# A decoder trunk whose split weight tiles lie at another shift in their buffers for each block of columns

## The chip, the cores and the metric

The kernel runs on one core of one Trainium2 chip. The metric is device time in microseconds (us), the median of repeated executions. Everything is float32, and no other core works beside it.

## The reference

The reference is a two-layer decoder trunk over 256 tokens of width 2048. Each layer has a mixing part (8 heads of sparse attention and 8 of stick-breaking attention, fed by one input projection and merged by one output projection) and a feed-forward part with a gate. Cut to what matters here:

```python
D_MODEL, SEQ, DEPTH, D_FF = 2048, 256, 2, 5632
for layer in range(DEPTH):
    xn = rms_norm(h, norm_mix[layer])
    h = h + hybrid_mixer(xn, ...)          # proj = xn @ w_in (2048 x 5656); ...; o @ w_out (2048 x 2048)
    xn = rms_norm(h, norm_ffn[layer])
    h = h + (silu(xn @ w_gate) * (xn @ w_up)) @ w_down    # 2048 x 5632, 2048 x 5632, 5632 x 2048
return rms_norm(h, norm_final)
```

The mixer also compresses keys and values by two small products (`w_cmp_k1`, `w_cmp_v1`, each 4096 x 256).

## The kernel before

All weights are read once, as 804 tiles of at most 128 x 1024 float32 (512 KB), in the order in which they are used (`plan`). A tile of 1024 columns holds two 512-column pieces for two steps of the inner dimension. Each tile goes through three stages, each in a ring of buffers:

- `load_next` (L150) has SyncE's queue bring tile i into one of `RAW` = 5 buffers `raw`. The load into a buffer waits until the split of the tile that was in it has been read to its end by VectorE.
- `split_next` (L159) cuts it into two parts whose sum is the float32 value and which TensorE multiplies in single passes: `hi` is a rounded copy by ScalarE (L165), `lo` the rest, `raw - hi`, by VectorE (L166). `hi` and `lo` have 4 buffers each. Up to `AHEAD` = 3 tiles are split ahead of the product that runs. Six tiles near the end are split into other places (`places`): buffers of `xh`/`xl` and `ah`/`al`.
- `mm` (L398) multiplies. The activations are the stationary operand, a 128 x 128 block of `xh`/`xl` (a transposed normalised input, split in the same way; for `w_down` it is `ah`/`al`), and the weights are the moving operand. For each 128 rows of weights and each half of the tokens three products go into the same accumulator: `xh*hi` (L409), `xh*lo` (L410), `xl*hi` (L411). `cmp_mm` (L540, L541) is the like for the two compressing products, with `fr`, 60 stationary columns per step, and 256 moving columns.

TensorE has one such stream of products from beginning to end. The attention, the norms and the transposes are generators, of which `step` runs one piece at every weight tile, so their instructions stand between the tiles' products. Instruction order is fixed by the program's text; no scheduler moves it.

Where the operands lie in a partition matters for this change. In the built program the tiles `xh`, `xl`, `raw`, `hi` and `lo` all start at addresses that leave 224 bytes when divided by 512; `ah` and `al` leave 96. Blocks and pieces inside the tiles start at multiples of 512 bytes, except in three kinds: the first block of columns of each layer is 280 wide, so its three pieces start 0, 1120 and 2240 bytes into the tile; the second is 256 wide; and step k of `fr` starts 240*k bytes into `fr`. In this document the *distance* of a product is the start of its moving operand less the start of its stationary operand, taken modulo 512. So `hi` with `xh` has distance 0, `hi` with `ah` has distance 128, the pieces of the first block have 0, 96 and 192, and `hi` with `fr` goes through all multiples of 16.

Of the kernel before, what the change touches and what calls it, by code (L numbers as in the profile page):

```python
# [8 lines left out]
F32R = mybir.dt.float32r  # L9
# [5 lines left out]
P = 128  # L15
# [9 lines left out]
EPS = 1e-6  # L25
NEG = -1e30
SCALE = 128 ** -0.5
EXPLN = "natural_log_exp_and_others"
SILU = "silu_and_others"

# the hidden columns of the feed-forward, in blocks of 512, are worked off in two parts
FF_PARTS = [(0, 6), (6, 11)]

# columns of the constants array
C_ID, C_NEG, C_CNEG, C_COK, C_D1, C_D0, C_MT, C_BM, C_INV, C_END = (
    0, 128, 384, 416, 448, 960, 1472, 1728, 1732, 1748)

# column blocks of the input projection, in the order in which they are computed
IN_CHUNKS = [
    ("ck", [(1024, 256), (2560, 24)]),  # L40
    ("cv", [(1280, 256)]),
# [20 lines left out]


def plan():
    """The tiles of one layer's weights in the order in which they are used."""

    def tiles(mat, name, cols, k1, k0=0):
        w = sum(c[1] for c in cols)
        step = max(1, min(4, 1024 // w))
        return [Item(mat, name, cols, list(range(k, min(k1, k + step))), k0, k1) for k in range(k0, k1, step)]  # L70

    main = {name: tiles("w_in", name, cols, KT) for name, cols in IN_CHUNKS}
    ck = tiles("w_cmp_k1", "wk", [(0, 256)], 32)
    cv = tiles("w_cmp_v1", "wv", [(0, 256)], 32)
    seq = []
    for name, _ in IN_CHUNKS:
        for j, t in enumerate(main[name]):
            seq.append(t)
            if name == "k" and ck and j >= 1:
                seq.append(ck.pop(0))  # L80
            elif name == "v" and j == 0:
                seq += ck
                ck = []
            elif (name == "v" and j >= 4) or name == "qn0":
                if cv:
                    seq.append(cv.pop(0))
    o = [tiles("w_out", f"o{c}", [(512 * c, 512)], KT) for c in range(4)]
    seq += o[0][:6] + o[1][:6] + o[0][6:] + o[1][6:] + o[2] + o[3]
    for c0, c1 in FF_PARTS:
        for c in range(c0, c1):  # L90
            for m, n in (("w_gate", "g"), ("w_up", "u")):
                seq += tiles(m, f"{n}{c}", [(512 * c, 512)], KT)
        for c in range(4):
            seq += tiles("w_down", f"d{c}", [(512 * c, 512)], 4 * c1, 4 * c0)
    off = 0
    for t in seq:
        t.off = off
        off += P * t.n
    return seq, off


def pi_parts(scale, bits, n):
    """2*pi*scale as n parts of `bits` leading bits each."""
    from fractions import Fraction
    rest = Fraction(2 * 314159265358979323846264338327950288419716939937510582097494459230781640628620899,
                    10 ** 80) * scale
    out = []
    for _ in range(n):
        e = 0
        while rest >= Fraction(2) ** (e + 1):  # L110
            e += 1
        while rest < Fraction(2) ** e:
            e -= 1
        q = Fraction(2) ** (e - bits + 1)
        part = (rest // q) * q
        out.append(float(part))
        rest -= part
    return out
# [3 lines left out]
def trunk(ctx: ExitStack, tc: tile.TileContext, x, positions, cst, gT, gfin, bgate, posT, w2, ws, out):  # L122
    nc = tc.nc
    V, A, T = nc.vector, nc.scalar, nc.tensor
    items, total = plan()
    seq = [(l, t) for l in range(DEPTH) for t in items]
# [4 lines left out]
    wp = ctx.enter_context(tc.tile_pool(name="wp", bufs=4))  # L131
# [10 lines left out]
    def o_ps():  # L142
        return ps.tile([P, 512], F32, tag="o", name="ops", bufs=1)

# [1 line left out]
    RAW, AHEAD = 5, 3  # L146
    raw, parts, places = {}, {}, {}
    ptr = [0, 0]

    def load_next():  # L150
        i = ptr[0]
# [7 lines left out]
    def split_next():  # L159
        i = ptr[1]  # L160
        n = seq[i][1].n
        r = raw.pop(i)
        hi, lo = places[i]() if i in places else (wp.tile([P, 1024], F32R, tag="hi", name="hi", bufs=4),
                                                  wp.tile([P, 1024], F32R, tag="lo", name="lo", bufs=4))
        A.activation(hi[:, :n], r[:, :n], AF.Copy)  # L165
        V.tensor_tensor(lo[:, :n], r[:, :n], hi[:, :n].bitcast(F32), op=OP.subtract)  # L166
        parts[i] = (hi, lo)
        ptr[1] += 1
# [6 lines left out]
        while ptr[0] < min(len(seq), ptr[1] + RAW):  # L175
            load_next()

# [1 line left out]
    active = []  # L179

    def spawn(g):
# [16 lines left out]

    flags = set()

# [1 line left out]
    cs = cp.tile([P, C_INV], F32, name="cs")  # L202
    inv = cp.tile([P, 16], F32, name="inv")
    gt = cp.tile([P, 3 * DEPTH, KT], F32, name="gt")
# [43 lines left out]
        nc.sync.dma_start(cs[:, P:], cst[:, P:C_INV])  # L248
        nc.sync.dma_start(w2t, w2)

# [1 line left out]
    cc = cp.tile([P, 3, 32], F32, name="cc")  # L252
    sn = cp.tile([P, 3, 32], F32, name="sn")

# [1 line left out]
    c2 = cp.tile([P, 3, 16], F32, name="c2")  # L256

    def angles():
        """positions * inv, brought into [-pi, pi] by an exact subtraction of whole turns."""
        G = nc.gpsimd  # L260
        MAGIC = 1.5 * 2.0 ** 23
        PI = 3.1415925
# [45 lines left out]
            A.activation(sn[:, :, sl], ang, AF.Sin, scale=2.0 * half - 1.0)  # L308

    def rope(X, tmp, idx, np_=P):  # L310
        """X [np_, n, 128], rotated in place by the tables' row idx."""
        n = X.shape[1]
        cb = cc[:np_, idx:idx + 1, :].to_broadcast([np_, n, 32])
        t = tmp[:np_, :2 * n * 32].rearrange("p (b n d) -> p b n d", b=2, n=n)
        V.tensor_tensor(t[:, 0], X[:, :, 0:32], cb, op=OP.mult)
        V.tensor_tensor(t[:, 1, :, 0:16], X[:, :, 16:32],
                        sn[:np_, idx:idx + 1, 0:16].to_broadcast([np_, n, 16]), op=OP.mult)
        V.tensor_tensor(t[:, 1, :, 16:32], X[:, :, 0:16],
                        sn[:np_, idx:idx + 1, 16:32].to_broadcast([np_, n, 16]), op=OP.mult)
        V.tensor_tensor(X[:, :, 0:32], t[:, 0], t[:, 1], op=OP.add)  # L320

# [1 line left out]
    def rsqrt_a(ss, v, r, count):  # L323
        V.tensor_scalar(v, ss, 1.0 / count, EPS, op0=OP.mult, op1=OP.add)

# [8 lines left out]
        V.tensor_tensor(r, r, q, op=OP.mult)  # L334

    class Norm:
        """1/rms of h per token, gathered block by block."""

        def __init__(self, parts=4):
            self.done = False  # L340
# [14 lines left out]
            rsqrt_c(v[:, :n], r, q[:, :n])  # L355
            self.done = True

# [1 line left out]
    def new_x():  # L359
        return [None] * 4  # L360

# [2 lines left out]
                xp.tile([P, 4, S], F32R, tag="xl", name="xl", bufs=5))  # L364

    def xt_block(X, c, srcs, g):
        """[tokens, 512 columns] times g per column, transposed into X[c]."""
        ts = []
        for t in range(2):
            src = srcs(t)  # L370
            pt = tmp_ps()
            for j in range(4):
                T.transpose(pt[:, j * P:(j + 1) * P], src[:, j * P:(j + 1) * P], ident)  # L373
            tv = tmp512().rearrange("p (a b) -> p a b", a=4)
            V.tensor_tensor(tv, pt.rearrange("p (a b) -> p a b", a=4),  # L375
                            g[:, 4 * c:4 * c + 4, None].to_broadcast([P, 4, P]), op=OP.mult)
            ts.append(tv)
        xh, xl = X[c]
        for t in range(2):
            A.activation(xh[:, :, t * P:t * P + P], ts[t], AF.Copy)  # L380
        for t in range(2):
            sl = slice(t * P, t * P + P)
            V.tensor_tensor(xl[:, :, sl], ts[t], xh[:, :, sl].bitcast(F32), op=OP.subtract)  # L383
# [12 lines left out]
        yield  # L396

    def mm(i, accs, X, ts=(0, 1)):  # L398
        """One weight tile: accs[t] += X^T[t] @ W, float32 by three passes."""
        it = seq[i][1]  # L400
        hi, lo = parts[i]
        for j, kt in enumerate(it.kts):
# [7 lines left out]
                T.matmul(o, a, lo[:, sl], start=False, stop=False)  # L410
                T.matmul(o, b, hi[:, sl], start=False, stop=(kt == it.k1 - 1))  # L411

    # =====================================================================
    norm = Norm()
    X = new_x()

# [25 lines left out]
    for l in range(DEPTH):  # L442
        g_mix, g_grp, g_ffn = gt[:, 3 * l, :], gt[:, 3 * l + 1, :], gt[:, 3 * l + 2, :]
        flags.clear()
        with ExitStack() as actx:
# [42 lines left out]
            flat = {}  # L488

            def c_chunk(which, accs):  # L490
                """Tokens of the compressed branch: transposed, cut into blocks, positions added."""
                while "prep" not in flags:
                    yield
                ns = []
# [101 lines left out]
                flags.add(which)  # L596

            def qk_chunk(name, accs):
                """Queries or keys: scaled, rotated where they are, transposed to [d, token]."""
                sc = rq if name[0] == "q" or name[:2] == "sq" else r  # L600
                ns = []
                for t in range(2):
# [26 lines left out]
                yield  # L629
                flags.add(name)  # L630

# [1 line left out]
            obank = {}  # L633

            def nsa_unit(g, rr, qi):
# [70 lines left out]
                         skip_group_check=True)  # L706

            def o_norm(qd, qi, o):
                """Each head's output over its root mean square."""
                if qd not in on:  # L710
                    on[qd] = big(f"on{qd}").rearrange("p (t d) -> p t d", t=2)
                dst = on[qd][:, qi]
# [40 lines left out]
                    yield from pipeline(us)  # L753
                flags.add("nsa")

# [1 line left out]
            def rev(a):  # L757
                s_, n_ = a.ap[-1]
                return bass.AP(tensor=a.tensor, offset=a.offset + (n_ - 1) * s_, ap=[*a.ap[:-1], [-s_, n_]])
# [49 lines left out]
            spawn(sb_driver(0))  # L809
            spawn(sb_driver(1))  # L810

# [1 line left out]
            ocmp = {}  # L813
            accs = None
            XO = new_x()
# [38 lines left out]
                parts.pop(pos)  # L854
                pos += 1

# [1 line left out]
            spawn(xt_gen(XO, 3, lambda t: on[3][:, t], g_grp, "on3"))  # L858
            norm = Norm()
            X = new_x()  # L860
# [35 lines left out]
                parts.pop(pos)  # L896
                pos += 1

# [1 line left out]
        with ExitStack() as fctx:  # L900
            fp = fctx.enter_context(tc.tile_pool(name=f"fp{l}", bufs=1))
            r = norm.r
# [92 lines left out]
                    step(active)  # L995
                step(active)
            else:
                # the last block of columns: one half of the tokens, whose rows leave beside the other half
                outs = out.rearrange("o (t p) d -> p (o t) d", p=P)
                accs = [acc(), acc()]  # L1000
                for t in range(2):
# [85 lines left out]
```

## Time and profile before

| | |
|---|---|
| median of 2 runs | 2322.35 us (2322.24 to 2322.46) |
| span of the profiled execution | 2320.4 us |
| TensorE (PE) busy | 2301.6 us, 99% of the span |
| VectorE (DVE) busy | 1331.5 us, 57% |
| ScalarE (ACT) busy | 1082.5 us, 47% |
| granted TensorE clock, mean | 0.999 |
| moved by DMA | 428.46 MB, mean 185 GB/s |

The span runs from the first to the last instruction of one profiled execution; what lies around it is the difference to the run times, some 2 us. Matmuls are pipelined: the duration that the profile gives for one is longer than the time between the starts of two, so the rate of TensorE is read from starts, not from durations.

### The profile page before, as it was taken

How to read it: one execution, taken by the hardware profiler on the slowest of the kernel's cores; microseconds unless marked ns; L12 is line 12 of the kernel's file. 1: busy time of each engine (PE TensorE's matmuls, PEld its weight loads, DVE VectorE, ACT ScalarE, POOL GpSimd, SP SyncE). 2: the span in 40 equal slices, each digit the busy share in tenths (PEclk: the TensorE clock that was granted, in tenths of full speed). 3: DMA queues.
4: the chain of work that ended last, by engine and by line, in shares of the span. 5: the costliest groups of instructions: out<-in, count | busy, mean ns of one | idle time of the engine just before them, and what ended most of it. 6: DMA issues, size and time to landing. Idle time of an engine off the chain costs nothing.

```text
span 2320.4 us, 28275 instructions
## 1 busy us (share of the span) xinstructions
PE 2301.6 (99%) x10842; PEld 1907.2 (82%) x10842; DVE 1331.5 (57%) x1766; ACT 1082.5 (47%) x1405; POOL 29.0 (1%) x59
## 2 busy tenths in 40 slices
PE   8999999999999999999999999999999999999998
PEld 7888888888888888888888888888888888888886
DVE  6766776655454445445567667765544544544554
ACT  6645554544443344444455455554444433444443
POOL 4000000000000000000000000000000000000000
PEclk9999999999999999999999999999999999999999
DMA  7854456666666666666567434456555555555553
GB/s 251 271 170 129 129 157 195 181 191 189 189 192 185 190 191 186 193 190 184 174 216 251 152 128 145 155 181 210 189 191 191 184 189 190 190 191 191 190 182 136
DMA packets 118824, 428.46 MB, mean 185 GB/s; under 512 B 13424, under 2 KB 13840, under 8 KB 118560
## 3 DMA queue, kind: packets, MB, share of 16 engines
q1 hardware_dynamic: 118464, 426.58, 58.4%
q8 instruction: 85, 1.39, 0.2%
q14 instruction: 51, 0.42, 0.0%
q0 software_dynamic: 224, 0.07, 0.0%
HBM read 424.50 MB, written 2.10 MB: 184 GB/s over the span
## 4 chain that ended last, share of the span: by engine, by line
PE 98%; DVE 1%; ACT 1%; DMA 0%; SPq 0%; issue 0%; ACTq 0%
PE acc L409 30%; PE acc L411 30%; PE acc L410 30%; PE ops L671 1%; PE tps L642 1%; PE tps L926 1%; PE tps L373 1%; PE ops L540 1%; PE ops L541 1%; PE tps L617 1%; PE ops L798 0%; PE tps L663 0%; DMA raw<-in_ws_dram 0%; PE tps L765 0%; PE ops L705 0%; PE tps L680 0%
## 5 line engine op out<-in xcount | busy, mean ns | idle before, releaser
L166 DVE TENSOR_TENSOR lo<-raw,hi 128x1024 fp32r<-128x1024 f32 (+1 forms) x798 | 970.9, 1221 | 825.0 <-ACT hi L165 823.6
L165 ACT ACTIVATE hi<-raw 128x1024 fp32r<-128x1024 f32 (+1 forms) x798 | 836.5, 1054 | 838.6 <-PE acc L411 827.4
L409 PE MATMUL acc<-hi,xh 128*128 128x512 f32 (+2 forms) x2432 | 954.9, 393 | 0.0
L411 PE MATMUL acc<-hi,xl 128*128 128x512 f32 (+2 forms) x2432 | 935.8, 385 | 0.0
L410 PE MATMUL acc<-lo,xh 128*128 128x512 f32 (+2 forms) x2432 | 935.2, 385 | 0.5 <-DVE lo L166 0.5
L411 PEld LDWEIGHTS acc<-hi,xl 128*128 128x128 f32 x2432 | 456.9, 188 | 91.8
L410 PEld LDWEIGHTS acc<-lo,xh 128*128 128x128 f32 x2432 | 457.6, 188 | 89.7 <-issue 3.3
L409 PEld LDWEIGHTS acc<-hi,xh 128*128 128x128 f32 x2432 | 457.5, 188 | 88.7 <-issue 3.3
L409 PE MATMUL acc<-hi,ah 128*128 128x512 f32 x680 | 269.3, 396 | 0.0
L411 PE MATMUL acc<-hi,al 128*128 128x512 f32 x680 | 268.4, 395 | 0.0
L410 PE MATMUL acc<-lo,ah 128*128 128x512 f32 x680 | 268.3, 395 | 0.0
L411 PEld LDWEIGHTS acc<-hi,al 128*128 128x128 f32 x680 | 128.1, 188 | 30.0
L410 PEld LDWEIGHTS acc<-lo,ah 128*128 128x128 f32 x680 | 128.2, 188 | 29.5
L409 PEld LDWEIGHTS acc<-hi,ah 128*128 128x128 f32 x680 | 128.1, 188 | 29.3
L929 ACT ACTIVATE ah<-tps 128x512 fp32r<-128x512 f32 x44 | 26.3, 598 | 83.0 <-PE tps L926 83.0
L930 DVE TENSOR_TENSOR al<-tps,ah 128x512 fp32r<-128x512 f32 x44 | 30.4, 692 | 55.3 <-ACT ah L929 55.3
L380 ACT ACTIVATE xh<-scr 128x512 fp32r<-128x512 f32 x48 | 29.2, 630 | 39.9 <-DVE scr L375 39.8
L665 ACT ACTIVATE pT<-tps 128x256 f32<-128x256 f32 (+1 forms) x32 | 15.7, 490 | 63.4 <-PE tps L663 63.4
L375 DVE TENSOR_TENSOR scr<-tps,gt 128x512 f32<-128x512 f32 x48 | 31.0, 685 | 21.7 <-PE tps L373 21.7
L911 ACT ACTIVATE sil<-acc,nr 128x512 f32<-128x512 f32 x44 | 29.9, 689 | 19.6 <-PE acc L411 19.6
L383 DVE TENSOR_TENSOR xl<-scr,xh 128x512 fp32r<-128x512 f32 x48 | 31.4, 693 | 4.9 <-ACT xh L380 2.9
L540 PE MATMUL ops<-hi,fr 128*60 128x256 f32 x128 | 31.7, 281 | 0.0
(197 smaller groups left out, 976.5 us busy)
## 6 DMA issues: line engine op xcount, KB each, us to landing
raw<-in_ws_dram SPq DMA_DIRECT2D x792, 512.0 KB, 3.6
raw<-in_ws_dram SPq DMA_DIRECT2D x10, 420.0 KB, 4.8
h<-in_x_dram SPq DMA_DIRECT2D x3, 512.0 KB, 8.3
gf<-in_gfin_dram SPq DMA_DIRECT2D x1, 1024.0 KB, 7.8
out_dram<-h SPq DMA_DIRECT2D x4, 256.0 KB, 2.3
out_dram<-h SPq DMA_DIRECT2D x2, 512.0 KB, 3.1
cs<-in_cst_dram SPq DMA_DIRECT2D x1, 802.0 KB, 5.8
h<-in_x_dram SPq DMA_DIRECT2D x2, 256.0 KB, 4.0
```

Of the source, the lines that this page charges most:

```text
L165: A.activation(hi[:, :n], r[:, :n], AF.Copy)
L166: V.tensor_tensor(lo[:, :n], r[:, :n], hi[:, :n].bitcast(F32), op=OP.subtract)
L375: V.tensor_tensor(tv, pt.rearrange("p (a b) -> p a b", a=4), g[:, 4 * c:4 * c + 4, None].to_broadcast([P, 4, P]), op=OP.mult)
L380: A.activation(xh[:, :, t * P:t * P + P], ts[t], AF.Copy)
L383: V.tensor_tensor(xl[:, :, sl], ts[t], xh[:, :, sl].bitcast(F32), op=OP.subtract)
L409: T.matmul(o, a, hi[:, sl], start=(kt == it.k0), stop=False)
L410: T.matmul(o, a, lo[:, sl], start=False, stop=False)
L411: T.matmul(o, b, hi[:, sl], start=False, stop=(kt == it.k1 - 1))
L540: T.matmul(o[:60, :256], fr[:, kt, :], hi[:, sl], start=(kt == 0), stop=False)
L911: A.activation(s, accs[t], AF.Silu, scale=r[:, t:t + 1])
L929: A.activation(ah[:, :, sl], pv, AF.Copy)
L930: V.tensor_tensor(al[:, :, sl], pv, ah[:, :, sl].bitcast(F32), op=OP.subtract)
```

## The change

`hi` and `lo` buffers grow from 1024 to 1152 columns, and the tile takes a window of 1024 in them that starts `at` columns in. All tiles of one block of columns (one accumulation) have the same `at`; the next block takes the next entry of `SHIFTS`: 0, 4, 8, ... 124 columns (steps of 16 bytes), then 2, 22, 42, 62, 82, 102, 122 (these start 8 bytes off a multiple of 16), then from the beginning. There are 48 blocks in a layer and 96 in all, so the 39 shifts are gone through about two and a half times. The six tiles with `places` keep their positions. To make room, the ring of `raw` buffers goes from 5 to 4. In the built program `xh`, `xl`, `hi` and `lo` buffers still leave 224 modulo 512 and `ah`, `al` still 96, so the distance of a product grows by the shift, modulo 512.

```diff
+SHIFTS = [4 * n for n in range(32)] + [4 * n + 2 for n in (0, 5, 10, 15, 20, 25, 30)]
...
-    RAW, AHEAD = 5, 3
+    RAW, AHEAD = 4, 3
...
+    chunks = []
+    for l_, t_ in seq:
+        if (l_, t_.mat, t_.name, t_.k0) not in chunks:
+            chunks.append((l_, t_.mat, t_.name, t_.k0))
+
+    def shift(i):
+        l_, t_ = seq[i]
+        n = chunks.index((l_, t_.mat, t_.name, t_.k0))
+        return SHIFTS[n % len(SHIFTS)]
...
-        hi, lo = places[i]() if i in places else (wp.tile([P, 1024], F32R, tag="hi", name="hi", bufs=4),
-                                                  wp.tile([P, 1024], F32R, tag="lo", name="lo", bufs=4))
+        if i in places:
+            hi, lo = places[i]()
+        else:
+            at = shift(i)
+            hi, lo = (wp.tile([P, 1024 + 128], F32R, tag=tag, name=tag, bufs=4)[:, at:at + 1024]
+                      for tag in ("hi", "lo"))
```

Of the 512-column products of line L409 to L411, 1,440 get a moving operand that starts 8 bytes off a multiple of 16, and 3,720 one that starts 16 bytes off a multiple of 32; before, all started at a multiple of 32.

The instructions of TensorE, VectorE, ScalarE and GpSimd stand in the same order as before. Only SyncE's queue differs, since the loads run one tile less far ahead. Near the start, before (`cs` holds constants, `w2t` small weights, the `raw` rows are weight tiles):

```order
L154 DMA raw<-in_ws_dram 128x840 x2
L154 DMA raw<-in_ws_dram 128x280
L154 DMA raw<-in_ws_dram 128x1024 x6
L248 DMA cs<-in_cst_dram 128x1604
L249 DMA w2t<-in_w_dram 128x1024
L154 DMA raw<-in_ws_dram 128x1024 x390
```

And with the change (its lines are 13 to 17 further down):

```order
L167 DMA raw<-in_ws_dram 128x840 x2
L167 DMA raw<-in_ws_dram 128x280
L167 DMA raw<-in_ws_dram 128x1024 x5
L265 DMA cs<-in_cst_dram 128x1604
L266 DMA w2t<-in_w_dram 128x1024
L167 DMA raw<-in_ws_dram 128x1024 x391
```

The loads of `cs` and `w2t` now stand ahead of one weight tile that they stood behind; the same holds for `gf` in the second layer.

## Rows read from the trace of the kernel before

**Rows 1.** The page, busy time by engine, and the granted clock in 40 slices

```profile
PE 2301.6 (99%) x10842; PEld 1907.2 (82%) x10842; DVE 1331.5 (57%) x1766; ACT 1082.5 (47%) x1405; POOL 29.0 (1%) x59
PEclk9999999999999999999999999999999999999999
```

**Rows 2.** The page, the chain that ended last, by engine

```profile
PE 98%; DVE 1%; ACT 1%; DMA 0%; SPq 0%; issue 0%; ACTq 0%
```

**Rows 3.** Groups by line and shape: count, busy us, mean ns, idle before

```profile
L409 PE MATMUL acc<-hi,xh 128*128 128x512 f32 x2304 | 917.4, 398 | 0.0
...
L409 PE MATMUL acc<-hi,ah 128*128 128x512 f32 x680 | 269.3, 396 | 0.0
```

**Rows 4.** Stretches, TensorE alone: from:to, us, busy (x matmuls), clock, DMA

```profile
616.70:649.30 32.60, 32.60 (x145) 1.00 0.66 196
706.00:828.00 122.00, 122.00 (x527) 1.00 0.64 189
1866.00:1977.00 111.00, 111.00 (x479) 1.00 0.57 189
```

**Rows 5.** Timeline of TensorE in an `xh` block: start us, duration us

```profile
620.09 0.39 PE L409 MATMUL acc<-hi,xh 128*128 128x512 f32 x1
...
623.49 0.39 PE L409 MATMUL acc<-hi,xh 128*128 128x512 f32 x1
```

**Rows 6.** The same in an `ah` block

```profile
710.05 0.39 PE L409 MATMUL acc<-hi,ah 128*128 128x512 f32 x1
...
712.14 0.40 PE L409 MATMUL acc<-hi,ah 128*128 128x512 f32 x1
712.38 0.40 PE L410 MATMUL acc<-lo,ah 128*128 128x512 f32 x1
...
713.30 0.39 PE L411 MATMUL acc<-hi,al 128*128 128x512 f32 x1
```

**Rows 7.** The same in the second layer's second block, 256 columns wide

```profile
1179.93 0.28 PE L409 MATMUL acc<-hi,xh 128*128 128x256 f32 x1
...
1181.73 0.28 PE L409 MATMUL acc<-hi,xh 128*128 128x256 f32 x1
```

**Rows 8.** The same in its first block, 280 columns wide

```profile
1172.30 0.29 PE L409 MATMUL acc<-hi,xh 128*128 128x280 f32 x1
...
1175.77 0.29 PE L409 MATMUL acc<-hi,xh 128*128 128x280 f32 x1
```

**Rows 9.** The same at two tiles of a compressing product

```profile
1207.80 0.28 PE L540 MATMUL ops<-hi,fr 128*60 128x256 f32 x1
...
1208.73 0.40 PE L409 MATMUL acc<-hi,xh 128*128 128x512 f32 x1
...
1215.16 0.28 PE L540 MATMUL ops<-hi,fr 128*60 128x256 f32 x1
...
1216.10 0.40 PE L409 MATMUL acc<-hi,xh 128*128 128x512 f32 x1
```

**Rows 10.** Groups by line and shape on VectorE and ScalarE

```profile
L166 DVE TENSOR_TENSOR lo<-raw,hi 128x1024 fp32r<-128x1024 f32 x786 | 959.7, 1225 | 819.4 <-ACT hi L165 818.2
...
L165 ACT ACTIVATE hi<-raw 128x1024 fp32r<-128x1024 f32 x786 | 827.0, 1058 | 832.3 <-PE acc L411 821.9 <-DVE lo L166 4.4 <-issue 2.4
...
L383 DVE TENSOR_TENSOR xl<-scr,xh 128x512 fp32r<-128x512 f32 x48 | 31.4, 693 | 4.9 <-ACT xh L380 2.9
```

**Rows 11.** Instructions on tile `fr`, VectorE's writes: min/median/max ns

```profile
L531 DVE TENSOR_TENSOR fr<-ft,fr x8: 657/658/659, 45.9 to 1230.9; 128x480 fp32r<-128x480 f32 x8
```

**Rows 12.** Weight loads issued from 85 to 112 us, then from 600 to 700 us

```profile
raw<-in_ws_dram SPq DMA_DIRECT2D x14, 512.0 KB, 4.6
...
raw<-in_ws_dram SPq DMA_DIRECT2D x35, 512.0 KB, 4.1
```

**Rows 13.** All waits of TensorE's matmuls on VectorE's splits: us, times, longest

```profile
PE acc L410 <- DVE lo L166: 0.5, 1, 0.5
```

## The prediction

> **What bounds the kernel now.** I read the page first. TensorE is busy for 2301.6 of 2320.4 us and its clock is granted in full, the 2.4 GHz level, in every slice [rows 1]; the chain that ended last is TensorE to 98% [rows 2]. In the whole run a matmul waited once, for 0.5 us, on a split of the weights [rows 13]. So the time is the sum of the distances between the starts of matmuls, and neither VectorE nor ScalarE nor the loads decide it as long as they stay hidden.
>
> The groups by line don't help with that sum: a 512-column product lasts 398 ns with `xh` and 396 ns with `ah` [rows 3], since products overlap. The starts do. In a quiet block with `xh` fifteen starts go from 620.09 to 623.49 us, 3.40 us / 15 = 226.7 ns each [rows 5], and 145 products touch a stretch of 32.6 us, so 32.6 / 144 = 226.4 [rows 4]. In the blocks of `w_down`, same shape, same lines, same full clock, fourteen starts take 713.30 - 710.05 = 3.25 us, 232.1 ns each [rows 6], and the long stretches give 122.0 / 526 = 231.9 and 111.0 / 478 = 232.2 [rows 4]. There is something between the two sorts of block that costs 5.3 ns in every product.
>
> What is unavoidable? 256 columns with `xh` take (1181.73 - 1179.93) / 15 = 120.0 ns [rows 7]. The 256 columns more of the wide product cost 226.7 - 120.0 = 106.7 ns, 0.417 ns per column, which is one column per period of 2.4 GHz. So 512 columns need 213.3 ns, and a fixed 13.4 ns goes with each product at distance 0; with `ah` at distance 128 it is 18.7 ns. The 280-wide block, whose distances are 0, 96 and 192 in turn, needs (1175.77 - 1172.30) / 27 = 128.5 ns [rows 8], fixed part 128.5 - 116.7 = 11.8 ns, as an average of the three. The compressing products run through the multiples of 16; two of their 32 tiles of eight products each give 0.93 / 8 = 116.3 and 0.94 / 8 = 117.5 ns [rows 9], fixed part 9.6 to 10.8 ns, though with 60 stationary columns instead of 128.
>
> **The change part by part.** *Products with `xh`.* 2,304 per line, 6,912 in all [rows 3], now stand at distance 0 and 226.7 ns. Spread over all distances they cost, at one measured end, 226.7 again, and at the other measured end, distance 128, 232.0. Neither end is a bound: single starts in the `ah` block are up to 712.38 - 712.14 = 0.24 us apart [rows 6], and nothing goes below 213.3. The middle of the two measured distances is 229.3. The compressing products, which average over all distances, have a smaller fixed part than either end, and so has the 280-wide block, so I go below the middle and take 228.5, 1.8 ns up: 6,912 x 1.8 = +12.4 us. The bounds that I keep for the range are 226 and 233: -5 to +44 us.
>
> *Products with `ah`.* 680 per line, 2,040 in all [rows 3], at 232.0 and distance 128 today. They go to the same average: 2,040 x (228.5 - 232.0) = -7.1 us, bounds -12 to +2. (The six tiles that keep their places are not counted; they don't change.)
>
> *The narrow products*, 384 with `xh` and 256 with `fr`, are at several distances already; at 1 ns each either way they are worth less than 1 us. I take 0.
>
> *Starts off 16 bytes.* 1,440 of the products above get a moving operand that starts 8 bytes off a line of 16. No row shows this for TensorE; the nearest is the stationary operand `fr`, at odd multiples of 16, which has no visible surcharge [rows 9]. I take 0, because the stream is contiguous after its first column. The upper bound is that every piece is fetched twice, 1,440 x 213.3 = +307 us, which I treat as a rival. The Trainium skill ("SBUF — State Buffer", Specifications) gives memory lines of 16 bytes and a penalty for each crossing to a new line; 512 columns that start 8 bytes off touch 129 lines instead of 128, an estimate of under 1% for those products, some 2 us, which is well inside my bounds.
>
> *The writes of the split.* ScalarE and VectorE now write at the shifted addresses, 1058 and 1225 ns per tile [rows 10]. VectorE writes the second halves of `fr` 8 bytes off a multiple of 16 already: 658 ns for 480 columns [rows 11], 1.37 ns per column, beside 693 / 512 = 1.35 ns at aligned places [rows 10]. So nothing is added. The cover is large: a tile of twelve products lasts 12 x 226.7 = 2.72 us and both engines wait for TensorE or for each other most of the time (832.3 and 819.4 us of idling in front of the splits [rows 10]). Without the cover it would be 786 splits at whatever they grow by.
>
> *Four `raw` buffers.* A load may start one tile later than now; SyncE's queue holds only loads behind it. In the feed-forward 35 tiles are loaded in 100 us, 2.86 us each [rows 12]. A ring of four lasts 11.4 us; of that the split takes 1.06 + 1.23 = 2.3 and the load 4.1 us [rows 12], so 5.0 us are spare. The tight place is the stretch of the compressing products: 14 loads in 27 us, 1.93 us each, landing after 4.6 us [rows 12]. Five buffers last 9.6 us and leave 2.7 spare; four last 7.7 and leave 7.7 - 2.3 - 4.6 = 0.8. Still positive, and behind it stand three tiles split ahead, some 5 us. If the spare time were negative by 1 us per tile over the 2 x 16 tiles there and the lead didn't cover it, it would be some 30 us. I take +0.5, bounds 0 to 6. The two loads that move ahead of one weight tile (`cs`, `w2t`) delay it once near the start, in the same lead; what is late next there would be ScalarE's split of that tile. No wait is added for anyone but SyncE.
>
> The sum is +12.4 - 7.1 + 0.5 = +5.8 us on the span of 2320.4, so 2326.2; the median of the runs lies 2322.35 - 2320.4 = 1.95 us above the span, which gives 2328 us. With the bounds of all parts on one side it would be 2305 or 2374, which is the range of this case alone.
>
> **The rivals.** *Addresses play no part.* The `ah` blocks could be slow for another reason (another region of memory, other work beside them). For it: only two distances are known in pure 512-column blocks, which is little. Against it: clock, shape and lines are the same in both. Then only the ring of `raw` changes, and the time is 2322.35 + 0.5 = 2323 us. By a rule of the Trainium skill ("TensorE: Matmul & The Clock Gate", Part 2) it should come out so: TensorE has two independent read ports, one for the moving operand and one for weight loads, and loading the next weights takes no bandwidth from the running matmul. The difference of 226.7 to 232.0 stays without an explanation by that rule.
>
> *Distance 0 is the good case (slower).* At distance 0 the starts keep an even beat of 226.7; at 128 they are uneven, from about 0.21 to 0.24 us [rows 6]. If every shift breaks the even beat and some do worse than 128 does, the average may lie halfway from 232.0 to the longest single start, 236: 6,912 x 9.3 + 2,040 x 4.0 = +72 us, 2395 us. It is over 2% from an average of 233.1 ns on. Against it speaks the small fixed part in rows 8 and 9.
>
> *Off-line starts are read twice (slower by much).* +307 us for the 1,440 products, 2635 us; from 32 ns more for each of them it passes 2%. Against it: nothing in a contiguous stream has to be fetched twice.
>
> *The aligned starts are the bad case (faster).* 0 and 128 are both multiples of 128; if other distances lose half as much, 6.7 of 13.4 and some 12 less than the 18.7, it is -46 - 24 = -70 us, 2252 us. For it: the smaller fixed parts of rows 8 and 9. Against it: 11.8 ns in the block that is at 96 and 192 for two thirds is far from half.
>
> *The loads come late.* In the compressing stretches the spare 0.8 us isn't there, and the lead of three tiles is used up: +12 to +20 us, some 2340 us.
>
> **How the numbers follow.** The sum has a chance of 0.48, addresses without effect 0.17, distance 0 as the good case 0.15, the fast case 0.09, off-line starts read twice 0.06, late loads 0.05. The predicted time is that of the sum, 2328 us. The range goes from 2285 to 2400: it leaves out the double reading (0.06), some half of the fast case (0.05) and a third of the slow one (0.06). Two per cent, 46 us, is about what a measurement of this kernel can tell from no change: below 2276 lies most of the fast case, 0.07; above 2369 the double reading, most of the slow case and an edge of the sum, 0.18; within 2%, 0.75.
>
> **What the changed profile would show.** Blocks differ in their distance between starts, each block uniform, and the same for equal distances: that is the mechanism, and its average is the term of 228.5. The blocks of `w_down` should lose their common 232. If all blocks with `xh` stay at 226.7 and those with `ah` at 232, addresses have no part. Blocks with shifts of 2, 22, 42 ... columns at over 400 ns would be the double reading. TensorE waits on ScalarE's split, or ScalarE on loads of `raw`, between 85 and 120 us and between 1195 and 1260 us would be the late loads. The prediction is wrong above all if the average over the distances isn't between 226 and 233 ns.

## The result and the profile after

The changed kernel takes 2358.36 us (2358.08 to 2358.63, 2 runs), the kernel before 2322.35. The ratio is 1.0155 with an interval of 1.0138 to 1.0172: slower by 36 us, clear of no change, though under the 2% named ahead. It lies 30 us above the predicted 2328 and inside the range of 2285 to 2400.

The page of the changed kernel, busy time by engine, granted clock, and the chain that ended last (its lines stand 13 to 17 further down than before):

```profile
PE 2337.2 (99%) x10842; PEld 1909.6 (81%) x10842; DVE 1332.4 (57%) x1766; ACT 1084.2 (46%) x1405; POOL 28.8 (1%) x59
...
PEclk9999999999999999999999999999999999999999
...
PE 96%; ACT 1%; DVE 1%; DMA 1%; issue 0%; SPq 0%; ACTq 0%
```

Beside [rows 1] the 35.9 us that the span grew (2356.3 after 2320.4) are all but 0.3 in TensorE's busy time, 2337.2 - 2301.6 = 35.6 us: TensorE is idle for 19.1 us of the span now and was for 18.8. So the chain's 96%, after 98% [rows 2], means only that the chain passes over a load or a split more often, not that TensorE waits more. The clock is granted in full as before, the counts are the same, and VectorE and ScalarE are as busy as before. So the same matmuls at the same clock follow one another more slowly.

The timeline of TensorE shows which. Start in us, duration in us; first the block with a shift of 256 bytes (distance 256), then the one of 400 bytes (distance 400), both with `xh`; then a block of `w_down` with 8 bytes (distance 136), and a block with `xh` at 8 bytes (distance 8):

```profile
387.85 0.39 PE L427 MATMUL acc<-lo,xh 128*128 128x512 f32 x1
...
397.82 0.39 PE L426 MATMUL acc<-hi,xh 128*128 128x512 f32 x1
...
592.98 0.40 PE L426 MATMUL acc<-hi,xh 128*128 128x512 f32 x1
...
602.78 0.40 PE L426 MATMUL acc<-hi,xh 128*128 128x512 f32 x1
...
774.44 0.41 PE L428 MATMUL acc<-hi,al 128*128 128x512 f32 x1
...
784.27 0.40 PE L428 MATMUL acc<-hi,al 128*128 128x512 f32 x1
...
1714.03 0.40 PE L427 MATMUL acc<-lo,xh 128*128 128x512 f32 x1
...
1723.83 0.40 PE L427 MATMUL acc<-lo,xh 128*128 128x512 f32 x1
```

44 starts take 9.97 us in the first, 226.6 ns each, the old rate of [rows 5]. In the others 42 starts take 9.80, 9.83 and 9.80 us: 233.3, 234.0 and 233.3 ns. Worked out from the start times of all 512-column products that follow another within 300 ns, the average with `xh` went from 227.5 to 232.6 ns and with `ah` from 232.4 to 232.9. By distance, only the four blocks at 0 and 256 average 227.0 to 228.1 ns; all others lie between 229.0 and 236.3. A distance and the same distance plus 256 differ no more than blocks at one distance do among themselves, but that can be 3 ns: at 240 the blocks have 233.3 to 236.3. 6,912 x 5.1 + 2,040 x 0.5 = 35 + 1 us, which is the loss.

The ring of four shows, but not on TensorE. Waits, engine and line, what for, us in total, times, longest, first ScalarE's in the kernel before, then two of the changed kernel:

```profile
ACT hi L165 <- DMA raw<-in_ws_dram: 2.5, 3, 1.4
...
ACT hi L182 <- DMA raw<-in_ws_dram: 17.1, 22, 1.8
...
PE acc L427 <- DVE lo L183: 0.9, 2, 0.6
```

ScalarE's split waits 17.1 us for loads where it waited 2.5; TensorE's matmuls wait 0.9 us for splits where they waited 0.5 [rows 13].

### The profile page after: what moved, and what is told of

Same layout as the page of the kernel before. It is cut to its first block, busy times and chain, and to the rows that moved or that the text cites. A ratio compares the mean times of both kernels' runs of the same rounds, so it can differ in the third digit from the quotient of the medians.

```text
span 2356.3 us, 28275 instructions
## 1 busy us (share of the span) xinstructions
PE 2337.2 (99%) x10842; PEld 1909.6 (81%) x10842; DVE 1332.4 (57%) x1766; ACT 1084.2 (46%) x1405; POOL 28.8 (1%) x59
## 4 chain that ended last, share of the span: by engine, by line
PE 96%; ACT 1%; DVE 1%; DMA 1%; issue 0%; SPq 0%; ACTq 0%
PE acc L426 30%; PE acc L427 30%; PE acc L428 30%; PE ops L688 1%; PE tps L659 1%; PE tps L943 1%; PE tps L390 1%; DMA raw<-in_ws_dram 1%; PE ops L557 1%; ACT hi L182 1%; PE ops L558 1%; DVE lo L183 1%; PE tps L634 0%; PE ops L815 0%; PE tps L680 0%
## 5 line engine op out<-in xcount | busy, mean ns | idle before, releaser
L426 PE MATMUL acc<-hi,xh 128*128 128x512 f32 (+2 forms) x2432 | 966.2, 397 | 0.0
L427 PE MATMUL acc<-lo,xh 128*128 128x512 f32 (+2 forms) x2432 | 945.9, 389 | 0.9 <-DVE lo L183 0.9
L428 PE MATMUL acc<-hi,xl 128*128 128x512 f32 (+2 forms) x2432 | 946.3, 389 | 0.0
```

Source lines behind the costliest of these rows:

```text
L426: T.matmul(o, a, hi[:, sl], start=(kt == it.k0), stop=False)
```

## The experiments

The theory after the result: the only cost is the distance between the moving and the stationary operand, modulo 256 bytes. Rivals: the shorter ring; the place of the moving operand or the writes of the split at shifted addresses; the region or the neighbours of `ah`; starts that aren't at a multiple of 16 bytes. e3, e4, e5, e6 and e8 were timed once each; the kernel before ranged over 1.2 us in the 13 runs beside e1 to e4 (2321.84 to 2323.08), so a difference of 1 or 2 us in the time alone says nothing here.

**The ring alone (e1).** The kernel before with one edit:

```diff
-    RAW, AHEAD = 5, 3
+    RAW, AHEAD = 4, 3
```

> The kernel before with four raw buffers instead of five and nothing else; every weight tile keeps its place relative to the activations. Theory (the distance between moving and stationary start is the whole cost): 2322 to 2324 us, TensorE as in the kernel before, ScalarE waiting some 15 us more for loads of raw, all of it hidden. Rival (the shorter ring costs part of the 36 us): 2330 us or more, with TensorE waiting on splits in the stretches of the compressing products.

Measured: 2323.67 us beside 2322.56 of the kernel before on that chip, ratio 1.0006 (0.9996 to 1.0015). Its waits:

```profile
ACT hi L165 <- DMA raw<-in_ws_dram: 26.7, 27, 3.2
...
PEld acc L410 <- DVE lo L166: 1.6, 3, 0.8
```

ScalarE waits 26.7 us for loads, 24.2 more than before where 15 were expected, and TensorE's weight loads wait 1.6 us for splits. The 512-column products with `xh` keep their average of 227.5 ns. The ring costs about 1 us, which isn't told from nothing. The rival falls.

**`ah` and `al` brought to distance 0 (e2).** The kernel before with an unused tile of 128 bytes ahead of them, which moves `ah`, `al` and the small tiles of that region by 128 bytes and leaves `xh`, `xl`, `hi` and `lo` in their places:

```diff
+    pad = tmpp.tile([P, 32], F32, name="pad")
```

> The kernel before with one unused tile of 128 bytes per partition that moves ah and al so that their distance to hi and lo is 0 instead of 128; five raw buffers, no shifts. Theory (distance): the 2,112 products of w_down go from 232.2 to some 227.2 ns, -10.6 us, 2312 us. Rival (the w_down blocks are slow because of the region in which ah and al lie, or of the work beside them): 232 ns stays, 2322 us.

Measured: 2310.89 us, ratio 0.9950 (0.9933 to 0.9966), 11.7 us faster than the kernel before. The timeline of a `w_down` block, beside [rows 6]:

```profile
709.87 0.39 PE L411 MATMUL acc<-hi,ah 128*128 128x512 f32 x1
...
719.85 0.39 PE L413 MATMUL acc<-hi,al 128*128 128x512 f32 x1
```

44 starts in 9.98 us, 226.8 ns each after 232.1. The same products in the same place of the program, with nothing moved but addresses, are 5.3 ns faster, and the average of all with `ah` goes from 232.4 to 226.8. It is the fastest kernel of the study.

**One constant shift (e3).** Four raw buffers and all `hi` and `lo` tiles at 60 columns, 240 bytes:

```diff
+            hi = wp.tile([P, 1024 + 128], F32R, tag="hi", name="hi", bufs=4)[:, 60:60 + 1024]
+            lo = wp.tile([P, 1024 + 128], F32R, tag="lo", name="lo", bufs=4)[:, 60:60 + 1024]
```

> All hi and lo tiles at the one shift of 60 columns (240 bytes), four raw buffers; one distance for all products with xh, 240, and one for ah, 368. Theory (distance): the products with xh at the 234 to 235.5 ns that the blocks at 240 and 496 showed, those with ah at 231, so 2322 + 6,912 x 7 to 8 - 2,040 x 1.3 = 2368 to 2375 us, slower than the mixed shifts. Rival (it is the changing from block to block, or the ring, that costs): at one constant shift the time is back near 2322 us.

Measured: 2362.42 us, 6 below the expected interval and 40 above the kernel before. So the changing of the shift is not what costs. Timeline of TensorE, two blocks with `xh` (distance 240), two of `w_down` (distance 368), and the 256-wide block of the second layer (distance 240):

```profile
641.02 0.39 PE L413 MATMUL acc<-lo,xh 128*128 128x512 f32 x1
...
650.82 0.39 PE L413 MATMUL acc<-lo,xh 128*128 128x512 f32 x1
...
686.41 0.40 PE L414 MATMUL acc<-hi,xl 128*128 128x512 f32 x1
...
696.35 0.40 PE L414 MATMUL acc<-hi,xl 128*128 128x512 f32 x1
...
758.02 0.39 PE L412 MATMUL acc<-hi,ah 128*128 128x512 f32 x1
...
768.00 0.39 PE L414 MATMUL acc<-hi,al 128*128 128x512 f32 x1
...
1144.04 0.40 PE L413 MATMUL acc<-lo,ah 128*128 128x512 f32 x1
...
1153.98 0.39 PE L414 MATMUL acc<-hi,al 128*128 128x512 f32 x1
...
1200.86 0.28 PE L412 MATMUL acc<-hi,xh 128*128 128x256 f32 x1
...
1203.09 0.28 PE L413 MATMUL acc<-lo,xh 128*128 128x256 f32 x1
```

With 42, 42, 44, 43 and 19 starts these are 233.3, 236.7, 226.8, 231.2 and 117.4 ns. Two things were not expected. At one and the same distance there are several steady rates: with `xh` the undisturbed blocks of the feed-forward hold 233.3 or 236.7, and with `ah` most hold 226.8, the even beat of distance 0, while three of the first layer and the last one have 231. In the changed kernel both blocks at 112 and 368 with `ah` had 231.2. All products with `ah` average 227.6 ns here instead of the 231 expected, 2,040 x 3.4 = 7 us, which is about the missing 6. So distance 0 isn't the one good case, and the distance alone doesn't set the rate. What went before matters: by the start times of this run's feed-forward, a rate lasts over tiles and blocks and changes only where transposes stand between the products or the stationary operand goes over from `xh` to `ah` or back. The first layer's first `w_up` block holds 233.3 throughout, the next `w_gate` block goes over to 236.7 at its second and third tile, which have transposes between their products, and the next `w_up` block holds 236.7. What chooses the new rate no run shows. And in the 256-wide block the distance of 240 is faster than the distance 0 of [rows 7], 117.4 after 120.0 ns.

**All starts of whole columns (e4).** The changed kernel with

```diff
-SHIFTS = [4 * n for n in range(32)] + [4 * n + 2 for n in (0, 5, 10, 15, 20, 25, 30)]
+SHIFTS = list(range(64))
```

> The changed kernel with the shifts 0, 1, 2, ... 63 columns (steps of 4 bytes) instead of its list, so that every distance of whole columns below 256 bytes occurs. Theory (a distance of 0 modulo 256 is the one good case and alignment to 8 or 16 bytes plays no part): only shift 0 runs at 227 ns, all others at 229 to 237, the average over blocks of xh near 233, 2356 to 2364 us. Rival (starts off 16 bytes cost extra): odd shifts stand clearly above their even neighbours, 2370 us or more. Second rival (some other start is better than 0): a block below 226 ns.

Measured: 2358.11 us, in the expected interval. Two blocks with `xh`, at 100 bytes and at 108 bytes:

```profile
593.93 0.40 PE L426 MATMUL acc<-hi,xh 128*128 128x512 f32 x1
...
603.77 0.40 PE L428 MATMUL acc<-hi,xl 128*128 128x512 f32 x1
...
641.05 0.39 PE L427 MATMUL acc<-lo,xh 128*128 128x512 f32 x1
...
650.82 0.39 PE L428 MATMUL acc<-hi,xl 128*128 128x512 f32 x1
```

41 starts in 9.84 us are 240.0 ns, 43 in 9.77 us are 227.2. My theory was too simple here: the start within 16 bytes does matter. Worked out by block from the start times, starts one column past a multiple of 16 are the worst, 233.4 to 239.9 ns, on average 236.9. Starts three columns past one are at 227.4 to 231.7, on average 229.1, and nearly as good as distance 0 at 28, 60, 108, 156 and 316 (227.4 to 228.0 beside 226.7). Starts two columns past (8 bytes) average 233.2, those on a multiple of 16 other than 0 and 256 232.4. The gains and losses cancel: all products with `xh` average 232.7 ns, after 232.6 in the changed kernel. The first rival is right for one odd column in two, and its time wasn't reached. No block is below 226.7, so the second rival falls.

**Everything moved (e5), and the activations alone moved (e8).** e5 puts an unused tile of 96 bytes ahead of `xh`, so that all operands move together; e8 keeps that tile and adds 416 bytes behind `xl`, so that `raw`, `hi`, `lo`, `ah` and `al` move by a whole 512 bytes, keep their remainder modulo 512, and only `xh` and `xl` change theirs.

```diff
+    pad1 = hp.tile([P, 24], F32, name="pad1")
```
```diff
+    gp = ctx.enter_context(tc.tile_pool(name="gp", bufs=1))
+    pad2 = gp.tile([P, 104], F32, name="pad2")
```

> The kernel before with one unused tile of 96 bytes per partition ahead of xh, so that xh, xl, raw, hi, lo, ah and al all lie 96 bytes further and all distances stay. Theory (only the distance between the two operands counts): 226.7 ns with xh in quiet blocks and 232 with ah as before, 2322 us. Rival (the place of the moving operand in memory counts, since 96 bytes of shift cost 233 ns in the changed kernel): 233 ns with xh, some 2360 us.

> The kernel before with xh and xl 96 bytes further and everything behind them a whole 512 bytes further, so that raw, hi and lo keep their remainder and only the stationary operand moves: distance 416 (160 modulo 256) with xh, still 128 with ah. Theory (distance): some 234 ns with xh as the blocks at 160 and 416 showed, 6,912 x 6.5 = +45 us, 2367 us. Rival (the writes of the split at shifted addresses, or the place of the moving operand, cost): nothing of that moves here, 2322 us.

Measured: e5 2324.43 us, e8 2365.45 us, within 3 us of what the theory had (2322, 2367). In e5, a block with `xh`, then one of `w_down`:

```profile
629.97 0.39 PE L411 MATMUL acc<-lo,xh 128*128 128x512 f32 x1
...
639.95 0.39 PE L410 MATMUL acc<-hi,xh 128*128 128x512 f32 x1
...
713.98 0.40 PE L411 MATMUL acc<-lo,ah 128*128 128x512 f32 x1
...
723.78 0.40 PE L411 MATMUL acc<-lo,ah 128*128 128x512 f32 x1
```

In e8, a block with `xh`:

```profile
634.01 0.40 PE L414 MATMUL acc<-hi,xl 128*128 128x512 f32 x1
...
643.85 0.40 PE L414 MATMUL acc<-hi,xl 128*128 128x512 f32 x1
```

44 starts in 9.98 us, 226.8 ns, with both operands moved by 96 bytes; 42 in 9.84 us, 234.3 ns, with the stationary one alone moved. So neither the place of the moving operand nor the address that the split writes to is the cause: the loss is there when the weight tiles keep their remainder, and gone when both operands move. Of the 2 us of e5 above the kernel before, 1.5 lie in `w_down`: at the same distance of 128 its products average 233.2 ns where they had 232.4. Both rates occur at this distance with either place of `ah` (two blocks of e5 keep 232.3 and 232.5, one of e8 has 233.2), so this looks like another case of several steady rates; a small effect of the place itself isn't excluded.

**`lo` alone shifted (e6).** `hi` stays at distance 0, `lo` is at 60 columns; four raw buffers:

```diff
+            hi = wp.tile([P, 1024 + 128], F32R, tag="hi", name="hi", bufs=4)[:, 0:0 + 1024]
+            lo = wp.tile([P, 1024 + 128], F32R, tag="lo", name="lo", bufs=4)[:, 60:60 + 1024]
```

> hi stays at distance 0 to xh, lo alone is shifted by 60 columns (distance 240 with xh, 368 with ah); four raw buffers. Theory (each product pays for its own distance): only the products of lo with xh lose 7 to 8 ns, 2,304 x 7.5 = +17 us, 2340 us, starts behind them at 234 and the others at 227. Rival (an even beat of all three is what is lost): all three products of a block average 232 or more, 6,912 x 5 to 7, 2357 us or more.

Measured: 2382.47 us, the slowest kernel of the study and above both the theory (2340) and the rival's floor of 2357. The ends of a stretch with `xh`, then four starts in a row in a `w_down` block and the last of the stretch that they begin:

```profile
629.90 0.40 PE L413 MATMUL acc<-lo,xh 128*128 128x512 f32 x1
...
639.79 0.39 PE L413 MATMUL acc<-lo,xh 128*128 128x512 f32 x1
...
730.08 0.40 PE L414 MATMUL acc<-hi,al 128*128 128x512 f32 x1
730.32 0.39 PE L412 MATMUL acc<-hi,ah 128*128 128x512 f32 x1
730.55 0.43 PE L413 MATMUL acc<-lo,ah 128*128 128x512 f32 x1
730.81 0.40 PE L414 MATMUL acc<-hi,al 128*128 128x512 f32 x1
...
740.00 0.43 PE L413 MATMUL acc<-lo,ah 128*128 128x512 f32 x1
```

With `xh` 42 starts in 9.89 us are 235.5 ns, though two of three products are at distance 0. In `w_down` the start behind `lo` comes 0.26 us later, the others after 0.24 and 0.23; 41 starts in 9.92 us are 242.0. Over all blocks the products with `xh` average 234.0 ns and those with `ah` 241.0, though the two distances that `w_down` has here gave 232.4 (128, the kernel before) and 227.6 (368, e3) by themselves. The theory that each product pays for its own distance falls: the mixture is dearer than either distance, and the even beat of all three is lost, as the rival said.

**The shifts with five buffers (e7).** The changed kernel with its shifts modulo 64 columns and `RAW` = 5. Buffers of 1088 columns suffice then; they are 256 bytes longer than a multiple of 512, so that neighbours in a ring lie 256 bytes apart modulo 512. One line of the edit:

```diff
-        return SHIFTS[n % len(SHIFTS)]
+        return SHIFTS[n % len(SHIFTS)] % 64
```

> The changed kernel with its shifts taken modulo 64 columns (256 bytes) and five raw buffers instead of four. Theory (distances count modulo 256 bytes, the ring is free): as the changed kernel, 2355 to 2360 us. Rival (part of the loss comes from the shorter ring together with the shifts): 2350 us or less.

Measured: 2356.66 us, ratio to the kernel before 1.0149 (1.0132 to 1.0166), 1.7 us below the changed kernel, whose interval of 1.0138 to 1.0172 covers nearly the same. The averages are those of the changed kernel, 232.6 ns with `xh` and 232.9 with `ah`. So 256 bytes more or less are worth nothing, even from tile to tile, and the fifth buffer is worth nothing that can be told from noise.

## Why the prediction was right, and where it was off

**What bounds the kernel** was right: all of the loss is in the starts of TensorE's products, at a full clock.

**The term for `xh` was mis-sized.** The direction held, and so did the mechanism in this: the blocks differ in their distance between starts by where the operands lie, and the blocks of `w_down` lost their common 232 (they have 227.2 to 236.3). Equal distances, against the prediction, didn't always give equal rates (233.3 to 236.3 at 240). The size is +35 us instead of +12.4. The step that failed is taking 226.7 and 232.0 as two ends of a spread and going below their middle because "The compressing products, which average over all distances, have a smaller fixed part than either end". The average of 232.6 lies above both ends; even the middle of 229.3 would have been 3.3 ns short. That 232.6 lies inside the bounds of 226 and 233 is luck in part: no row gave 233 as a bound, and it held by 0.4 ns. Narrow products don't follow the wide ones: at distance 240 the 256-wide block takes 117.4 ns, less than the 120.0 at distance 0, while the 512-wide products at 240 take 233.3 or 236.7 instead of 226.7. The nearest row was that of the same shape at distance 128, 232.0 [rows 6], and it would have given 6,912 x 5.3 = +37 us.

**The term for `ah`** was -7.1 and came out at +1: with an average of 232.6 to 232.9 over the distances there was nothing to gain by leaving 128. The gain that was there needed distance 0 (e2, -11.7 us).

**Starts off 16 bytes**: 0 was taken for the 8-byte starts. Their products average 233.7 ns, those at the multiples of 16 other than 0 and 256 232.7, so it is 1.4 us for the 1,440 at most, and the distances differ as well. The double reading is excluded: no block is above 236.3. That 0 holds for all columns would have been wrong: e4 has 240.0 at 100 bytes.

**The writes** were hidden as said, and unchanged: the splits' mean durations are 1058 and 1225 ns per tile in the changed kernel too, as in [rows 10].

**Four `raw` buffers**: +0.5 taken, +1.1 measured in e1 (interval -0.9 to +3.5 us, from the ratio). The spare time in the compressing stretches wasn't always the 0.8 us worked out: of ScalarE's 17.1 us of waits for loads 6.8 lie between 85 and 120 us and 2.8 between 1195 and 1260 us, the prediction's sign of late loads. The lead of three tiles covered them, since TensorE's matmuls wait 0.9 us in all.

The sum with the measured terms is 35 + 1 + 1 = 37 us beside 36 measured.

**The rivals.** "Distance 0 is the good case" came nearest to what happened, with 0.15: in the changed kernel the blocks at 0 and 256 are the fastest. It priced the others too high, at an average of 236 instead of 232.6, and e3 and e4 show good cases beside 0. "The aligned starts are the bad case" is the reverse of what was measured. "Addresses play no part" is excluded by e2, e5 and e8: e8 takes 43 us more than the kernel before (2365.45 after 2322.19) with no remainder changed but that of the stationary operand. The rule of the Trainium skill that the prediction put beside it ("TensorE: Matmul & The Clock Gate", Part 2) says that TensorE has two independent read ports, so that loading the next weights takes no read bandwidth from the running matmul. What the prediction concluded from it, that addresses have no effect, doesn't hold here, and the measurement decides; whether the ports themselves are otherwise isn't shown. The weight loads' busy time is nearly the same before and after (1907.2 and 1909.6 us), so the loss doesn't show as longer loads. In which part of the chip the two operands' places come to matter together, and whether it is the block in use or the one being loaded for the next product that counts, no run tells apart.

## What to carry to other kernels

When a stream of matmuls is the bound and each has a new stationary block, read the time between starts by block, not the durations, and compare blocks of the same shape: a few ns between them may be nothing but the distance of two operands in memory, and an unused tile can take it away (128 bytes, 11.7 us here). To price a term, prefer the one row of the same shape in the other state to several rows of another shape. When several buffers are read in turn by one stream, give them all the same remainder; one of them alone at another cost most here (e6, 60 us).

## What was not expected of the hardware

The rate of a stream isn't a function of the distance alone: at distance 368 blocks ran at 226.8 or 231.2 ns, at 240 at 233.3 or 236.7, each for some hundred products on end. No block of products 512 columns wide averages below 226.7 ns in any run, 13.4 above what the columns take by the prediction's working. That floor is reached at distance 0, 256 and, in e3, 368, and nearly at some starts that lie 12 bytes past a multiple of 16 (227.2 at 108); two columns before that, at 100, it is 240.0. With 256 columns the order of the distances is another (117.4 at 240, 120.0 at 0).
